# Down products of a macaron trunk as seven block products for eight

## The chip, the cores and the metric

The kernel runs on one core of a Trainium2 chip. The core has TensorE (PE) for matrix products, VectorE (DVE), ScalarE (ACT) and GpSimd (POOL) for element work, SyncE (SP) for issuing DMAs, an on-chip memory SBUF and an accumulator memory PSUM of eight banks. The metric is the device time of one launch in microseconds (us).

## The reference: what is computed

Two layers work on 528 tokens of width 1024 (512 frames behind 16 learned meta tokens). Each layer is

```
h = h + 1/2 * SwiGLU_1(RMSNorm(h))
h = h + mixer(RMSNorm(h))           # stick-breaking attention, a convolution branch, gates, output projection
h = h + 1/2 * SwiGLU_2(RMSNorm(h))
SwiGLU(x) = (silu(x @ w_gate) * (x @ w_up)) @ w_down     # inner width 2816
```

and after the layers a last RMSNorm, with the meta tokens dropped. All arrays are float32. The inner width 2816 is 22 row tiles of 128, the width 1024 is 8 tiles of 128. The change touches the four SwiGLU blocks (FFNs) alone, in them chiefly the product with `w_down`.

## The kernel before

Everything lies transposed: channels on the 128 partitions, tokens along the free dimension, so `h` is eight tiles of 128x528. In the last FFN only the 512 frame tokens are computed (mode `XO`), in the other three all 528 (`FULL`).

**Precision.** A float32 product is made of three products of a cheaper type: `split` (lines 77 to 80) gives a high part (a ScalarE copy) and the rest (a VectorE subtraction), for weights (`wh`, `wl`) and activations (`uh`, `ul` and so on), and every product is high x high, high x low, low x high. So each weight tile costs ScalarE and VectorE work before TensorE may use it.

**Weights.** The list `units` holds all weight pieces in the order of use. `unit` (line 243) hands the next one out and prepares ahead, `LOOK` = 3 units beyond it; raw tiles come by DMA on SP's queue into three buffers (`wr`), the two parts go into four buffers each (`wh`, `wl`). Mixer weights get their low part in another way: ScalarE writes the negated raw tile, and a DMA on Pool's queue adds the raw weights to it in memory (lines 224 to 226).

**Gate and up.** Row tiles of gate and up are computed in pairs by `quad` (line 566). Weights are cut into 2x2 blocks (two halves of the 1024 inputs by the two row tiles), activations into 2x2 blocks (input halves by token halves). Seven block products take the place of eight, and sums before and after make up for it: weight sums s1 and s3 are built by a DMA that loads one block and a DMA on Pool's queue that adds the other (`fetch_sums`, line 196), s2 and s4 by a VectorE addition (line 236). The results gather in PSUM: A (tag `ps`, two tiles), B (`pb`, one tile, begun as a ScalarE copy of A), G (copied to SBUF as q), E (`pe`, one tile, begun by VectorE as q - B), and c22 = q - B in SBUF. `out` (lines 592 to 594) makes u = up * silu(gate * rstd) of each quarter. The first tiles of an FFN (two, in the first FFN four) are made by plain products (line 502).

**Down.** The 22 row tiles lie in four groups of 4, 6, 6 and 6. After the quads of a group, `down` (line 622) multiplies its tiles by `w_down`, for all eight output tiles of the width (line 260). For this `parts` (line 484) has split each u into `ah` and `al`. In the first three groups VectorE takes an output from PSUM, times 1/2 and times the norm's factor rstd (line 638), and Pool adds it to `h` (line 640). In the last group Pool multiplies u by rstd beforehand (line 486), VectorE adds to `h` directly (line 633), and `after` prepares the next stage's input from each finished tile of `h`. The first two outputs of a group are interleaved so that the tiles that are ready latest are used last.

**Order.** TensorE takes products in the order written. The other engines' instructions are put in order by a planner from priorities (the order of writing, moved by `priority(offset)`), and each engine then runs its list in order and waits at its head. The mixer's TensorE order is written out by hand and isn't touched.

## Time and profile before

| quantity | value |
|---|---|
| time, median of 3 runs | 2152.11 us (2151.22 to 2152.19) |
| span of the profiled execution | 2150.5 us |
| the profiled execution's own time beside its span | not given apart from the span; the median of the runs is 1.6 us above it |
| busy: PE, DVE, ACT, POOL | 2135.9, 1521.5, 1137.9, 488.7 us |
| a quad of gate and up, FULL | 20.4 us |
| a down stage of six tiles, FULL | 35.1 us |
| moved by DMA | 324.90 MB |

In rows of the profile, `wl<-wr,wh 128x1024` means that a tile wl of 128 partitions by 1024 elements is written from wr and wh; `xN` is a count; "mean ns" is the duration of one; the text in square brackets of a time row is the engine's idle time before it and what ended it. A window's row gives the busy time of each engine in that stretch, then TensorE's granted clock, the DMA engines' busy share and GB/s.

### The profile page before, as it was taken

How to read it: one execution, taken by the hardware profiler on the slowest of the kernel's cores; microseconds unless marked ns; L12 is line 12 of the kernel's file. 1: busy time of each engine (PE TensorE's matmuls, PEld its weight loads, DVE VectorE, ACT ScalarE, POOL GpSimd, SP SyncE). 2: the span in 40 equal slices, each digit the busy share in tenths (PEclk: the TensorE clock that was granted, in tenths of full speed). 3: DMA queues.
4: the chain of work that ended last, by engine and by line, in shares of the span. 5: the costliest groups of instructions: out<-in, count | busy, mean ns of one | idle time of the engine just before them, and what ended most of it. 6: DMA issues, size and time to landing. Idle time of an engine off the chain costs nothing.

```text
span 2150.5 us, 39932 instructions
## 1 busy us (share of the span) xinstructions
PE 2135.9 (99%) x16226; PEld 2052.8 (95%) x16226; DVE 1521.5 (71%) x2091; ACT 1137.9 (53%) x1587; POOL 488.7 (23%) x449
## 2 busy tenths in 40 slices
PE   9999999999999999999999999999999999999998
PEld 9999999999999999999999999999888889999897
DVE  7867685677766777677877676856677767767685
ACT  6434355467776545343554443554778775444354
POOL 1322321211111131313113223212112111322320
PEclk9999999999999999999999999999999999999999
DMA  8465536865578747464365655368656886665542
GB/s 236 133 165 141 142 104 198 181 138 119 134 169 180 175 129 189 129 161 122 99 169 145 168 140 146 103 193 184 142 127 133 187 188 167 159 175 143 144 111 77
DMA packets 140168, 324.90 MB, mean 151 GB/s; under 512 B 15568, under 2 KB 19664, under 8 KB 139984
## 3 DMA queue, kind: packets, MB, share of 16 engines
q1 hardware_dynamic: 101856, 226.36, 33.3%
q0 software_dynamic: 37440, 95.44, 26.1%
q8 instruction: 127, 2.08, 0.4%
q10 hardware_dynamic: 688, 0.55, 0.1%
q14 instruction: 57, 0.47, 0.1%
HBM read 315.86 MB, written 6.42 MB: 150 GB/s over the span
## 4 chain that ended last, share of the span: by engine, by line
PE 99%; ACT 0%; DVE 0%; DMA 0%; issue 0%; DVEq 0%; ACTq 0%
PE pb L580 16%; PE ps L580 16%; PE ps L720 15%; PE ps L260 12%; PE ps L706 10%; PE pe L260 6%; PE pb L260 6%; PE pe L580 5%; PE z L706 2%; PE ps L502 2%; PE pe L502 1%; PE pb L502 1%; PE z L877 1%; PE po L921 1%; PE z L900 1%; PE ps L554 1%
## 5 line engine op out<-in xcount | busy, mean ns | idle before, releaser
L79 ACT CAST wh<-wr 128x1024 fp32r<-128x1024 f32 (+4 forms) x275 | 242.2, 887 | 372.4 <-PE ps L260 94.5
L80 DVE TENSOR_TENSOR wl<-wr,wh 128x1024 fp32r<-128x1024 f32 (+4 forms) x275 | 300.6, 1096 | 57.4 <-ACT wh L79 53.5
L79 ACT CAST wh<-s 128x1024 fp32r<-128x1024 f32 x158 | 165.8, 1049 | 274.9 <-DVE s L236 83.1
L80 DVE TENSOR_TENSOR wl<-s,wh 128x1024 fp32r<-128x1024 f32 x158 | 216.1, 1368 | 59.4 <-ACT wh L79 58.7
L720 PE MATMUL ps<-uh,wh 128*128 128x264 f32 (+1 forms) x792 | 243.8, 308 | 0.0
L720 PE MATMUL ps<-uh,wl 128*128 128x264 f32 (+1 forms) x792 | 240.0, 303 | 0.0
L720 PE MATMUL ps<-ul,wh 128*128 128x264 f32 (+1 forms) x792 | 239.9, 303 | 0.0
L640 POOL TENSOR_TENSOR h<-h,dt 128x528 f32<-128x528 f32 (+1 forms) x96 | 179.9, 1879 | 258.1 <-DVE dt L638 255.2
L210 POOL DMA_DIRECT2D s<-wg x78 | 72.8, 938 | 596.9 <-DMA s<-wg 337.9
L748 DVE SCALAR_TENSOR_TENSOR y<-uc,prm,y 128x528 f32<-128x528 f32 (+1 forms) x240 | 197.7, 824 | 4.1
L224 ACT CAST wh<-wr 128x1024 fp32r<-128x1024 f32 x104 | 109.1, 1049 | 141.2 <-issue 46.9
L580 PE MATMUL ps<-ul,wh 128*128 128x264 f32 (+1 forms) x624 | 177.4, 284 | 0.0
L580 PE MATMUL pb<-sl,wh 128*128 128x264 f32 (+1 forms) x624 | 176.9, 283 | 0.0
L580 PE MATMUL ps<-uh,wl 128*128 128x264 f32 (+1 forms) x624 | 176.9, 283 | 0.0
L580 PE MATMUL pb<-sh,wl 128*128 128x264 f32 (+1 forms) x624 | 176.8, 283 | 0.0
L580 PE MATMUL pb<-sh,wh 128*128 128x264 f32 (+1 forms) x624 | 176.5, 283 | 0.0
L580 PE MATMUL ps<-uh,wh 128*128 128x264 f32 (+1 forms) x624 | 176.2, 282 | 0.0
L720 PEld LDWEIGHTS ps<-uh,wl 128*128 128x128 f32 x792 | 149.1, 188 | 5.9
L720 PEld LDWEIGHTS ps<-uh,wh 128*128 128x128 f32 x792 | 148.9, 188 | 5.4
L720 PEld LDWEIGHTS ps<-ul,wh 128*128 128x128 f32 x792 | 149.0, 188 | 5.1
L260 PE MATMUL ps<-ah,wh 128*128 128x264 f32 (+1 forms) x616 | 142.0, 300 | 0.0
L260 PE MATMUL ps<-ah,wl 128*128 128x264 f32 (+1 forms) x616 | 141.8, 300 | 0.0
(319 smaller groups left out, 6460.8 us busy)
## 6 DMA issues: line engine op xcount, KB each, us to landing
wr<-wd SPq DMA_DIRECT2D x96, 384.0 KB, 3.6
wr<-win SPq DMA_DIRECT2D x72, 512.0 KB, 4.4
wl<-win POOLq DMA_DIRECT2D x72, 512.0 KB, 7.8
wr<-wg SPq DMA_DIRECT2D x117, 256.0 KB, 3.0
wr<-wu SPq DMA_DIRECT2D x117, 256.0 KB, 3.4
s<-wg SPq DMA_DIRECT2D x78, 256.0 KB, 5.2
s<-wu SPq DMA_DIRECT2D x78, 256.0 KB, 5.7
s<-wg POOLq DMA_DIRECT2D x78, 256.0 KB, 5.2
```

The source lines that it names most:

```text
L79: act.copy(hi, x)
L80: dve.tensor_tensor(out=lo, in0=x, in1=f(hi), op=ALU.subtract)
L210: pool.dma_start(t[:, a:b], src, accum_op=ALU.add)
L224: act.copy(hi[:, :nk], raw[:, :nk])
L260: pe.matmul(ps[:, c, :n], wt[:, k0 + k, :], xt[:, s:s + n], start=(k == 0 and pi == 0), stop=(k == end and pi == 2))
L502: pe.matmul(ps[:, e, :TH], wt[:, k, :], xt[:, s], start=(k == ORDER[0] and pi == 0), stop=(k == ORDER[-1] and pi == 2))
L554: pe.matmul(ps[:, e, :TH], wt[:, k, :], xt[:, s], start=(k == 0 and pi == 0), stop=(k == KD - 1 and pi == 2))
L580: pe.matmul(ps[:, e, :TH], wt[:, 4 * e + kk, :], xt, start=start and kk == 0 and pi == 0, stop=kk == 3 and pi == 2, skip_group_check=True)
L640: pool.tensor_tensor(out=tri(h[j], mode), in0=tri(h[j], mode), in1=tri(t, mode), op=ALU.add)
L706: pe.matmul(ps, wt[:, k0 + k, :], xt[:, s], start=(n == 0 and pi == 0), stop=(n == nk - 1 and pi == 2))
L720: pe.matmul(ps, wt[:, k, :], xt[:, s], start=(n == 0 and pi == 0), stop=(n == KD - 1 and pi == 2))
L748: t = dve.scalar_tensor_tensor(out=y, in0=uc[i][:, c0 + k:k + T], scalar=col(w0 + k), in1=y, op0=ALU.mult, op1=ALU.add)
```

## The change

- The groups become three of 6 tiles and one of 4. A pair of row tiles in `quad` is now tile i and tile i + 3 of a group (in the last group neighbours as before).
- In the first three groups `down_quads` takes the place of `down`: the six row tiles as two halves of three, the outputs as two halves of four, the tokens as two halves, seven products instead of eight, for two sets d of 2x2 output tiles. One product is 3 tiles x 3 parts x 2 output tiles = 18 matmuls of half the tokens. Weight sums are made as in `quad`, of 128x768, with loads of 1536 contiguous bytes per partition and output tile.
- The activations of a pair are split in seven halves: one half (`first_part`), one whole tile (`second_part`), and four half sums made by VectorE in place in the u tiles (`sum_ops`), split as two whole tiles (`sum_parts`) or, for the last pair of a group, one half at a time in the order of use (`sum_halves`). They stay in SBUF in 20 buffers (`ap`) and the `nsum` tile.
- u is multiplied by rstd beforehand in all groups, by Pool (`normed`), by VectorE for the last quarter of a group's last pair. `h` stays in SBUF throughout: an output leaves PSUM by ScalarE, times 1/2, and Pool adds its two half rows to `h` (`give`).
- Urgent operations get priority by `URGENT` = 200. The tags g, nt and dt share three buffers; s3, q and c22 have one buffer instead of two; the loads of s1 and s3 are issued apart from each other.
- The last group keeps `down`, with four tiles.

```diff
-GROUPS = ((0, 4), (4, 10), (10, 16), (16, 22))
-PLAIN, PLAIN_FIRST = 2, 4
+GROUPS = ((0, 6), (6, 12), (12, 18), (18, 22))
+NH = 3
+PAIRS = tuple(tuple((m0 + i, m0 + NH + i) for i in range(NH)) for m0, _ in GROUPS[:-1]) + (((18, 19), (20, 21)),)
+PLAIN, PLAIN_FIRST = 1, 2
...
+URGENT = 200
...
+    DOWN = ((0, "w11"), (1, "w11"), (0, "s1"), (0, "s2"), (0, "w21"), (0, "s3"), (0, "w22"), (0, "s4"),
+            (1, "s1"), (1, "s2"), (1, "w21"), (1, "s3"), (1, "w22"), (1, "s4"))
...
+                if gi < len(GROUPS) - 1:
+                    units += [((n, fi, l, ("d", gi, d)), (wd[l], m0, d), n) for d, n in DOWN]
+                else:
+                    units += [((f"d{fi}", l, gi, j), wd[l, j, :, m0:m1], m1 - m0) for j in ORDER]
...
+    SUM_BUFS = {"s1": 2, "s3": 1}
...
+            if is_down(n):
+                w, m0, d = src
+                j = 4 * c + 2 * d
+                return [(0, 2 * NH, w[j:j + 2, :, m0 + NH * k:m0 + NH * k + NH].rearrange("j p k c -> p j k c"))]
...
-            if nk == "w11":
-                fetch_sums()
+            size = 2 * NH if is_down(n) else 8
+            if nk in ("s1", "w22"):
+                fetch_sums("s1" if nk == "s1" else "s3")
             if nk in ("s2", "s4"):
-                x, y = raws[("s1", *at)], raws[("w22" if nk == "s2" else "w21", *at)]
+                x, y = (raws[(e, *at)][:, :size] for e in ("s1", "w22" if nk == "s2" else "w21"))
                 dve.tensor_tensor(out=x, in0=x, in1=y, op=ALU.add)
-            split(raws[("s1" if nk in ("s2", "s4") else nk, *at)], hi, lo)
+            raw = raws[("s1" if nk in ("s2", "s4") else nk, *at)][:, :size]
+            split(raw, hi[:, :size], lo[:, :size])
...
+                return fp.tile([P, T], F32, tag="nt", bufs=3, name="g")
...
+            def normed(eng, u, s):
+
+                eng.tensor_tensor(out=u[:, s], in0=u[:, s], in1=norm["r"][:, s], op=ALU.mult)
...
             def parts(u, m):
-                if m >= GROUPS[-1][0]:
-                    pool.tensor_tensor(out=tri(u, mode), in0=tri(u, mode), in1=tri(norm["r"], mode), op=ALU.mult)
-                ah = fp.tile([P, T], F32R, tag="ah", bufs=6, name="ah")
-                al = fp.tile([P, T], F32R, tag="al", bufs=6, name="al")
+                normed(pool, u, both)
+                ah, al = (fp.tile([P, T], F32R, tag="ap", bufs=20, name=n) for n in ("ah", "al"))
...
+            def first_part(p, ua):
+                t = two(slot(p, 0), mode)
+                split(ua[:, toks[0]], t[:, 0], t[:, 1])
+                a_parts["w11", p] = (t[:, 0], t[:, 1])
+
+            def whole_part(p, n, u, names):
+                hi, lo = slot(p, n), slot(p, n + 1)
+                split(tri(u, mode), tri(hi, mode), tri(lo, mode))
+                for name, s in zip(names, toks):
+                    a_parts[name, p] = (hi[:, s], lo[:, s])
+
+            def second_part(p, ub):
+                whole_part(p, 1, ub, ("w21", "s4"))
+
+            def sum_ops(ua, ub):
+
+                t1, t2 = toks
+                return ((ub[:, t2], ua[:, t2], ub[:, t2], ALU.subtract), (ua[:, t2], ua[:, t1], ua[:, t2], ALU.subtract),
+                        (ua[:, t1], ub[:, t2], ua[:, t1], ALU.subtract), (ub[:, t1], ub[:, t1], ua[:, t1], ALU.add))
+
+            def sum_halves(p, ua, ub):
+
+                places = (("s1", 3, 1), ("s3", 5, 1), ("s2", 5, 0), ("w22", 3, 0))
+                tiles = {n: slot(p, n) for n in range(3, 7)}
+                ops = sum_ops(ua, ub)
+                for n in (0, 1, 2, 3):
+                    o, x, y, op = ops[n]
+                    name, at, t = places[n]
+                    dve.tensor_tensor(out=o, in0=x, in1=y, op=op)
+                    a_parts[name, p] = tuple(tiles[at + e][:, toks[t]] for e in range(2))
+                    split(o, *a_parts[name, p])
+
+            def sum_parts(p, ua, ub):
+                for o, x, y, op in sum_ops(ua, ub):
+                    dve.tensor_tensor(out=o, in0=x, in1=y, op=op)
+                whole_part(p, 3, ub, ("w22", "s1"))
+                whole_part(p, 5, ua, ("s2", "s3"))
...
                 B = ptile("pb")
-                act.copy(v(B), v(A))
+                with priority(-URGENT):
+                    act.copy(v(B), v(A))
                 G = ptile()
                 products(G, "s1", sx(0), True)
-                q = sp.tile([P, 2, TH], F32, tag="q", bufs=2, name="q")
-                act.copy(q, v(G))
-                while late:
-                    parts(*late.pop())
+                q = sp.tile([P, 2, TH], F32, tag="q", bufs=1, name="q")
+                with priority(-URGENT):
+                    act.copy(q, v(G))
                 products(B, "s2", sx(1))
                 E = ptile("pe")
-                dve.scalar_tensor_tensor(out=v(E), in0=v(B), scalar=-1.0, in1=q, op0=ALU.mult, op1=ALU.add)
+                with priority(-URGENT):
+                    dve.scalar_tensor_tensor(out=v(E), in0=v(B), scalar=-1.0, in1=q, op0=ALU.mult, op1=ALU.add)
+                while late:
+                    late.pop()()
                 products(A, "w21", x(0, 1))
                 out(A, 0, 0)
+                if not last:
+                    normed(pool, u[0], toks[0])
                 products(B, "s3", sx(2))
-                c22 = sp.tile([P, 2, TH], F32, tag="c22", bufs=2, name="c22")
-                dve.scalar_tensor_tensor(out=c22, in0=v(B), scalar=-1.0, in1=q, op0=ALU.mult, op1=ALU.add)
+                c22 = sp.tile([P, 2, TH], F32, tag="c22", bufs=1, name="c22")
+                with priority(-URGENT):
+                    dve.scalar_tensor_tensor(out=c22, in0=v(B), scalar=-1.0, in1=q, op0=ALU.mult, op1=ALU.add)
                 products(E, "w22", sx(3))
+                if not last:
+                    first_part(p, u[0])
                 out(c22, 1, 1)
                 out(E, 1, 0)
-                parts(u[1], m + 1)
+                if last:
+                    parts(u[1], m + 1)
+                else:
+                    normed(pool, u[1], both)
                 products(B, "s4", x(1, 1))
-                out(B, 0, 1)
-                late.append((u[0], m))
-
-            def down(gi, tp=None):
+                with priority(-URGENT):
+                    out(B, 0, 1)
+                if last:
+                    late.append(lambda: parts(u[0], m))
+                elif p < NH - 1:
+                    normed(pool, u[0], toks[1])
+                    late.append(lambda: (second_part(p, u[1]), sum_parts(p, *u)))
+                else:
+                    late.append(lambda: (second_part(p, u[1]), normed(dve, u[0], toks[1]), sum_halves(p, *u)))
+
+            def down_quads(sp, gi):
+                with priority(-URGENT):
+                    late.pop()()
+
+                def products(ps, name, d, start=False):
+                    hi, lo = unit(name, fi, l, ("d", gi, d))
+                    for k in range(NH):
+                        xh, xl = a_parts[name, k]
+                        for pi, (wt, xt) in enumerate(((hi, xh), (hi, xl), (lo, xh))):
+                            for e in range(2):
+                                pe.matmul(ps[:, e, :TH], wt[:, NH * e + k, :], xt, start=start and k == 0 and pi == 0,
+                                          stop=k == NH - 1 and pi == 2, skip_group_check=True)
+
+                def v(t):
+                    return t[:, :, :TH]
+
+                def give(src, c, t, d):
+
+                    dt = two(fp.tile([P, T], F32, tag="nt", bufs=3, name="dt"), mode)
+                    with priority(-URGENT):
+                        act.activation(dt, src, AF.Copy, scale=0.5)
+                    for e in range(2):
+                        hj = h[4 * c + 2 * d + e][:, toks[t]]
+                        pool.tensor_tensor(out=hj, in0=hj, in1=dt[:, e], op=ALU.add)
+
+                def opposite(out, B, q):
+                    with priority(-URGENT):
+                        dve.scalar_tensor_tensor(out=out, in0=v(B), scalar=-1.0, in1=q, op0=ALU.mult, op1=ALU.add)
+
+                As = []
+                for d in range(2):
+                    As.append(ptile())
+                    products(As[d], "w11", d, True)
+                for d, A in enumerate(As):
+                    B = ptile("pb")
+                    with priority(-URGENT):
+                        act.copy(v(B), v(A))
+                    G = ptile("pe")
+                    products(G, "s1", d, True)
+                    q = sp.tile([P, 2, TH], F32, tag="q", bufs=1, name="q")
+                    with priority(-URGENT):
+                        act.copy(q, v(G))
+                    products(B, "s2", d)
+                    E = ptile("pe")
+                    opposite(v(E), B, q)
+                    products(A, "w21", d)
+                    give(v(A), 0, 0, d)
+                    products(B, "s3", d)
+                    c22 = sp.tile([P, 2, TH], F32, tag="c22", bufs=1, name="c22")
+                    opposite(c22, B, q)
+                    products(E, "w22", d)
+                    give(c22, 1, 1, d)
+                    give(v(E), 1, 0, d)
+                    products(B, "s4", d)
+                    give(v(B), 0, 1, d)
+
...
-                    t = fp.tile([P, T], F32, tag="nt", bufs=3, name="dt")
-                    dve.scalar_tensor_tensor(out=sv(t, mode), in0=pv(pd, mode), scalar=0.5, in1=sv(norm["r"], mode),
-                                             op0=ALU.mult, op1=ALU.mult)
-                    pool.tensor_tensor(out=tri(h[j], mode), in0=tri(h[j], mode), in1=tri(t, mode), op=ALU.add)
+                    dve.scalar_tensor_tensor(out=sv(h[j], mode), in0=pv(pd, mode), scalar=0.5, in1=sv(h[j], mode),
+                                             op0=ALU.mult, op1=ALU.add)
...
+                for gi, group in enumerate(PAIRS):
+                    for p in range((PLAIN_FIRST if first else PLAIN) if gi == 0 else 0, len(group)):
+                        quad(sp, gi, p)
                     if gi < len(GROUPS) - 1:
-                        down(gi)
+                        down_quads(sp, gi)
```

The start of the first FFN and the plain start of the others hand their tiles to the same functions; the last FFN's squares use a shared buffer.

131 lines of the change are left out of this document (76 added, 55 removed).

## The prediction

> **What bounds the kernel now.** I read the page's head first, then whom TensorE waits for, then the chain of waits, then the stages by windows.
>
> ```profile
> span 2150.5 us, 39932 instructions
> ...
> PE 2135.9 (99%) x16226; PEld 2052.8 (95%) x16226; DVE 1521.5 (71%) x2091; ACT 1137.9 (53%) x1587; POOL 488.7 (23%) x449
> ...
> PE 99%; ACT 0%; DVE 0%; DMA 0%; issue 0%; DVEq 0%; ACTq 0%
> ```
> ```profile
> PE ps L554 <- ACT wh L79: 4.8, 1, 4.8
> ```
> The end is set by TensorE alone: the chain stays on it, and its only wait of note is the 4.8 us before the first product. So a change is worth the matmul time it takes out, less the new holes it makes. The chain in order of time gives the price of a matmul:
>
> ```profile
> 368.33 5.83 PE z L706 x48
> ...
> 839.09 5.82 PE ps L580 x48
> ...
> 1052.41 8.78 PE ps L260 x72
> ...
> 1087.56 5.83 PE pb L502 x48
> ...
> 1898.72 5.69 PE ps L580 x48
> ...
> 1918.62 8.34 PE ps L260 x36
> ```
> A 264-column matmul costs 0.121 us (5.82/48) in block products (line 580) and 0.122 in down products (line 260). In the last FFN, where the meta tokens are dropped, a 256-column one costs 0.1185 and a 512-column one 0.2317. The windows show what else is loaded while TensorE runs full at clock 1.00: a quad of a middle group, a quad of the last group, a down stage, the start of the next FFN.
>
> ```profile
> 915.10:935.50 20.40, 20.40 (x171) 20.40 (x170) 16.13 (x22) 10.81 (x16) 3.24 (x4) 1.00 0.62 160
> 1011.50:1032.00 20.50, 20.50 (x171) 20.50 (x170) 18.22 (x22) 11.15 (x16) 3.51 (x2) 1.00 0.32 86
> 955.96:991.10 35.14, 35.14 (x290) 35.14 (x290) 19.58 (x21) 8.41 (x11) 13.99 (x7) 1.00 0.36 104
> 1060.50:1091.50 31.00, 31.00 (x256) 31.00 (x255) 30.96 (x49) 22.54 (x36) 0.00 (x0) 1.00 0.37 116
> ```
> After span, columns are PE, PEld, DVE, ACT, POOL. VectorE is second: 16 to 18 of 20.4 us in a quad, and wholly busy for 31 us between two FFNs without one hole in TensorE.
>
> **The change, part by part. TensorE.** Per FFN the down products of 18 tiles in a full FFN were 8x18x6 = 864 matmuls; they become 3 groups of 14 products of 18, 756. 108 fewer at 0.1213 are 13.1 us, three times: 39.3. In the last FFN 8x22x3 = 528 of 512 columns (122.3 us) become 756 of 256 (89.6) and 96 of 512 (22.2): 10.5. Together 49.8 us. Gate and up keep their 39 quads. The matmul count doesn't move: 3x108 fewer, 324 more.
>
> **VectorE in a quad.** Its prices are the spacing of starts where it doesn't wait:
>
> ```profile
> 916.06 1.22 DVE L236 TENSOR_TENSOR s<-s,wr 128x1024 f32<-128x1024 f32 x1
> 917.20 0.70 DVE L80 TENSOR_TENSOR al<-up,ah 128x528 fp32r<-128x528 f32 x1
> 917.81 0.43 DVE L594 TENSOR_TENSOR up<-pb,g 128x264 f32<-128x264 f32 x1
> 918.16 1.22 DVE L80 TENSOR_TENSOR wl<-wr,wh 128x1024 fp32r<-128x1024 f32 x1
> 919.29 1.22 DVE L80 TENSOR_TENSOR wl<-s,wh 128x1024 fp32r<-128x1024 f32 x1
> ```
> ```profile
> 854.46 0.96 DVE L80 TENSOR_TENSOR wl<-wr,wh 128x768 fp32r<-128x768 f32 x1
> 855.34 0.43 DVE L592 TENSOR_TENSOR g<-c,rstd 128x264 f32<-128x264 f32 x1
> ```
> So 1.14 for 1024 columns, 0.88 for 768, 0.62 for 528, 0.35 for 264. A quad now takes nine of 1.14, four of 0.62 and eight of 0.35: 15.5. The change replaces two residual splits (1.24) by one half split, three whole ones and four half sums (0.35 + 1.86 + 1.40 = 3.6): 17.9. To this comes Pool, which now multiplies both row tiles by the norm (2x264 and 528 columns). What that does, the last group shows already:
>
> ```profile
> 1012.41 1.33 POOL L486 TENSOR_TENSOR up<-up,rstd 128x528 f32<-128x528 f32 x1 [2.46 <-DVE up L594]
> 1015.93 2.18 POOL L486 TENSOR_TENSOR up<-up,rstd 128x528 f32<-128x528 f32 x1 [2.19 <-DVE up L594]
> ```
> ```profile
> 1012.52 2.31 DVE L236 TENSOR_TENSOR s<-s,wr 128x1024 f32<-128x1024 f32 x1
> ...
> 1016.84 2.35 DVE L80 TENSOR_TENSOR wl<-s,wh 128x1024 fp32r<-128x1024 f32 x1
> ```
> Beside a Pool operation of 1.33 a VectorE one of 1.22 takes 2.31 to 2.35: they go one after the other. Two of them made the quad's VectorE time 18.22 instead of 16.13, 2.1 more. So the second and third quad of a group need 17.9 + 2.1 = 20.0 of TensorE's 20.4. The first of a group needs 3.3 less, 16.7: what is left of a pair (second split, sums) is issued inside the next quad, and the third pair's goes to the down stage.
>
> **VectorE in a down stage**, which lasts 252x0.1213 = 30.6 us. 14 weight splits and 4 weight sums at 0.88, 4 opposites at 0.62: 18.3; the last pair's rest, with its own norm, 3.9. The outputs cost it nothing more: they go by ScalarE (14 weight casts, 4 copies and 8 outputs by the rows below: 14x0.84 + 12x0.59 = 18.8 of 30.6 us).
>
> ```profile
> L79 ACT CAST wh<-wr 128x768 fp32r<-128x768 f32 x96 | 79.1, 836 | 162.1 <-PE ps L260 48.9 <-issue 38.8 <-PE pe L260 27.9
> ...
> L603 ACT COPY q<-ps 128x528 f32<-128x528 f32 x29 | 17.2, 592 | 0.0
> ```
> But Pool adds 16 halves of 264 columns. Such an operation isn't in the trace: between half of 1.33 and all of it; I take 0.7, nearest in work to the half. That is 11.2 us, of which between none and all delays VectorE; I take 7, since some two thirds of its stage is on operations of two SBUF inputs. Then 29.2 of 30.6. A group of three quads and a down stage: 16.7 + 2x20.0 + 29.2 = 85.9 of TensorE's 91.8 us. It fits, at 94%, with little room in three of four stages. I charge holes between 0 and 6.6 us a group (the upper end is the slow rival's, below) and take 0.9, nearer the bottom because the 31 us of full VectorE above made no hole: 12 groups, 10.8.
>
> **Shared pair.** The Trainium skill, "SBUF — State Buffer", section "SBUF: two separate sides", has this pair of ports as an exclusive lock held for a whole instruction, the later one blocked fully. The 2.31 and 2.35 agree. By it all of Pool's time would fall on VectorE whenever that is never idle, which is the slow rival.
>
> **Last group, four tiles instead of six.** The first two outputs start with the tiles that are ready, which covers the last quad's late rest. Cover falls from 60 matmuls (7.3 us) to 36 (4.4).
>
> ```profile
> 1052.45 0.43 DVE L592 TENSOR_TENSOR g<-pb,rstd 128x264 f32<-128x264 f32 x1 [0.86 <-PE pb L580]
> ...
> 1057.85 0.71 DVE L80 TENSOR_TENSOR al<-up,ah 128x528 fp32r<-128x528 f32 x1 [2.10 <-ACT ah L79]
> ...
> 1060.49 0.71 DVE L633 SCALAR_TENSOR_TENSOR h<-ps,h 128x528 f32<-128x528 f32 x1 [1.93 <-PE ps L260]
> ...
> 1090.13 0.76 DVE L319 SCALAR_TENSOR_TENSOR ul<-h,prm,uh 128x528 fp32r<-128x528 f32 x1
> ```
> The rest was ready at 1058.6, 6.2 after the stage began at 1052.4: 1.8 late, unless the new priority of that output hastens it. 0 to 1.8, take 0.9, four times: 3.6.
>
> **Into the mixer (twice).** The stage's outputs now take 24 matmuls (2.9 us) each instead of 36 (4.4), and weights are prepared three units ahead.
>
> ```profile
> 355.05 1.06 ACT L224 CAST wh<-wr 128x1024 fp32r<-128x1024 f32 x1 [2.13 <-PE ps L260]
> ```
> ```profile
> 357.36 0.88 POOL L226 DMA_DIRECT2D wl<-win  x1 [19.30 <-ACT wl L225]
> ```
> ```profile
> DMA to landing us min/median/max: 8.0/8.2/8.9
> ```
> The first mixer weight began at 355.05, 13.3 before its use at 368.33; its low part was issued at 357.36 and landed 8.2 to 8.9 later, near 366. Three units are now 8.8 us, 4.5 less, so it lands about 2.2 late, with 0.5 covered by the high products: 0 to 2.2, take 1.7, twice: 3.4.
>
> **Between the FFNs (once).** VectorE had 31 us of work from 1060.5; the last input half (1090.13) was done at 1090.9 and needed at 1087.56 + 7/8x5.83 = 1092.7. TensorE now comes 11.7 earlier; VectorE starts 2.9 earlier and saves about 2.3 (eight weight splits a third shorter than 0.88): late by 5 at most, 0 if the deferred sums give way; take 2.6.
>
> **Loads and queues.** A down stage issues 14 transfers of 384 KB for 8, four of them accumulations on Pool's queue. Each accumulation waits there until its plain load has landed; behind it stand the output adds, which hold the three tiles of the tag that outputs, g tiles and sums now share, and for these ScalarE's outputs wait. Four outputs come in 15 us and the adds of one last 1.4, so a block of 4 us on Pool is covered; the cost if not is in the handover rival. The single q and c22 cost nothing: their last readers are done a product or more before the next write, behind w11 and s1. The single s3 buffer leaves six products, 13.1 us, between the two output pairs of a down stage, for a 384 KB load and its accumulation; the 512 KB accumulation above takes 8.2 and
>
> ```profile
> wr<-wd SPq DMA_DIRECT2D x96, 384.0 KB, 3.6
> ```
> makes 11.8; issue adds some 1 to 2. A delay of 1 us is hidden by the three products of preparation; uncovered it is 12 us in all, one per group. I take nothing.
>
> **Sum**: 2150.5 - 49.8 + 10.8 + 3.6 + 3.4 + 2.6 = 2121.1. The page gives this execution only its span; the median of the runs, 2152.11, lies 1.6 above, and I add that: 2122.7.
>
> **The rivals.** *Nearly all hidden* (0.18): only the mixer's entry costs: 2152.1 - 49.8 + 3.4 = 2105.7. For it: the full 31 us without a hole. Against: Pool's blocking was not there.
>
> *Handovers in the down stage* (0.13): a product now covers 18 matmuls, 2.2 us, where a quad's had 2.9. In that time the opposite must read the one pb tile: an operation under way (0.9, or up to 2.3 when blocked) and its own 0.7. Three such places in each of 24 output pairs, 0.5 us each, are 36 instead of 10.8: 2147.9. For it: one pb and one pe tile. Against: the new priorities put these operations first.
>
> *VectorE becomes the bound* (0.16): the slower side. If every Pool operation blocks it (2.8 in a quad, 11.2 in a down stage) and a quarter of the 4.3 us it idles in the 915.1 quad can't be filled, the second and third quads take 21.8 instead of 20.4 and the down stage 34.4 instead of 30.6: 2.8 + 3.8 = 6.6 a group, 79 in all: 2150.5 - 49.8 + 9.6 + 79 + 1.6 = 2190.9. It decides from a need above 20.4 a quad; I put it at 20.0. The lock rule above makes this time if it is read strictly.
>
> *The matmuls saved aren't time saved* (0.03): the 3024 new block matmuls would have to cost 0.0165 more each, 0.138, to eat the 49.8; at half of that the time is 2147.6. Against: lines 260 and 580, one with banks in alternation as here, cost 0.122 and 0.121.
>
> **How the numbers follow.** The forecast has 0.50: 2122.7, its own range 2108 to 2142. Some 0.2% (4 us) is about what the measurement tells from none. Faster takes the forecast, the hidden case and half of the handovers and of the last rival: 0.76; within 0.2%: 0.07, from their other halves; slower: 0.17. For 8 in 10 the range reaches from 2104 to 2158, leaving out the bottom of the hidden case and most of the VectorE-bound one.
>
> **What would show it.** PE still x16226 with some 2086 us of work; DVE about 2415 instructions; down stages of 30.6 to 33 us; waits of TensorE on VectorE of 1 us and less, most in the second and third quads and at the opposites. Wrong: quads above 21 us (VectorE bound), down stages above 34, or a mixer entry without a hole.

## The result, and the profile after

The changed kernel takes 2311.47 us (2302.48 to 2318.72, four runs) against 2151.66 for the kernel before beside it: ratio 1.074, 95% interval 1.0712 to 1.0767. The prediction said 2122.7, 2104 to 2158. The sign is wrong and the time is far outside the range.

The head of the page of the changed kernel, and the first line of its chain of work:

```profile
span 2316.9 us, 41061 instructions
...
PE 2164.1 (93%) x16214; PEld 2077.1 (90%) x16214; DVE 1739.5 (75%) x2415; ACT 1299.4 (56%) x1899; POOL 648.0 (28%) x676
...
PE 21%; DVE 4%; DMA 3%; issue 2%; ACT 1%; POOL 1%; POOLq 0%; SPq 0%; DVEq 0%; ACTq 0%
```
VectorE has exactly the 2415 instructions of the forecast. But TensorE is idle for 2316.9 - 2164.1 = 152.8 us, where the forecast's sum leaves 2121.1 - 2086.1 = 35.0, and busy for 2164.1 instead of some 2086. The two differences, 117.8 and 78.0, make up all of 2316.9 - 2121.1 = 195.8.

Next, busy times by stage for one group of the second FFN: its three quads, then its down stage. Kernel before:

```profile
798.10:859.40 61.30, 61.30 (x507) 61.30 (x506) 48.33 (x61) 31.06 (x43) 13.40 (x14) 1.00 0.68 171
859.40:894.50 35.10, 35.10 (x289) 35.10 (x289) 19.54 (x21) 8.29 (x11) 14.01 (x7) 1.00 0.35 109
```
The changed kernel (the columns are the stretch, its length, busy time and instructions of TensorE, its weight loads, VectorE, ScalarE and Pool, the granted clock, the DMA share, GB/s):

```profile
885.70:960.40 74.70, 66.50 (x506) 66.08 (x505) 53.88 (x73) 33.83 (x49) 27.54 (x26) 0.91 0.62 143
960.40:994.90 34.50, 32.89 (x255) 32.48 (x254) 26.08 (x34) 19.38 (x30) 19.29 (x19) 0.95 0.67 175
```
In this group the time is lost in the gate and up quads, whose products the change leaves as they were: 74.7 us for 61.3. The down stage, which it rewrites, takes 34.5 for 35.1. VectorE is busy for 53.88 of the 74.7, so it isn't full. The clock is 0.91 in the quads.

The waits of TensorE in the changed kernel (us in total, times, longest):

```profile
PE pb L672 <- ACT pb L692: 76.5, 27, 5.6
PE pe L742 <- ACT ap L82: 20.2, 12, 2.4
PE pb L742 <- DVE pe L759: 9.4, 9, 1.5
PE pb L742 <- ACT pb L768: 5.4, 4, 2.4
```
Half of the idle time is one wait: a quad's s2 product waits for ScalarE's copy of the tile A into the tile B. Two large waits of other engines lead there:

```profile
POOL s L235 <- DMA s<-wg: 217.2, 34, 28.2
ACT ap L82 <- POOL up L513: 198.3, 68, 6.4
```
Pool stands before an accumulation until its plain load has landed, and ScalarE stops for Pool's multiplication of u by rstd. One such place in the changed kernel, by its timeline, in order of time (the bracket is the idle time just before, and what ended it):

```profile
170.82 1.20 POOL L235 DMA_DIRECT2D s<-wd  x1 [6.91 <-DMA s<-wd]
171.56 1.25 POOL L513 TENSOR_TENSOR up<-up,rstd 128x264 f32<-128x264 f32 x1
172.84 0.41 ACT L82 CAST ap<-up 128x264 fp32r<-128x264 f32 x1 [5.02 <-POOL up L513]
173.16 0.42 ACT L106 ACTIVATE g<-g 128x264 f32<-128x264 f32 x1
173.29 0.43 DVE L83 TENSOR_TENSOR ap<-up,ap 128x264 fp32r<-128x264 f32 x1 [4.13 <-ACT ap L82]
178.44 2.85 POOL L513 TENSOR_TENSOR up<-up,rstd 128x528 f32<-128x528 f32 x2 [5.64 <-DVE up L686]
180.62 0.63 ACT L82 CAST ap<-up 128x528 fp32r<-128x528 f32 x1 [2.20 <-POOL up L513]
182.11 0.59 ACT L692 COPY pb<-ps 128x528 f32<-128x528 f32 x1
182.75 0.59 PE L672 MATMUL pb<-sh,wh 128*128 128x264 f32 x1 [4.23 <-ACT pb L692]
```
Pool waits 6.91 us for a plain load, because the next thing in its queue is the accumulation onto it. The multiplication behind it starts at 171.56, and ScalarE has stood 5.02 us at the split that reads the product. Behind that split stand the silu at 173.16 and, in the end, the copy. Later in the quad the second tile takes the way VectorE, Pool, ScalarE with a Pool that had nothing to do: 2.20 us more at ScalarE's head. Of these 7.2 us some 3.0 are absorbed, and 4.23 become a hole in TensorE.

This place is not a single case. In the first three FFNs the timeline has 14 quads in which a wait behind an accumulation (4.0 to 6.4 us) and a second one of 2.2 us come before the same copy. In each of them TensorE's hole is the sum of the two less 2.9 to 3.0 us; together these holes are 61.2 of the 76.5 us. In the last group of each FFN a wait of 2.1 to 2.2 us comes alone before a copy, and no hole follows.

After the hole TensorE's matmuls are slow. The same place in stretches of 3 us:

```profile
179.00:182.00 3.00, 0.00 (x0) 0.00 (x0) 1.49 (x4) 1.38 (x2) 2.29 (x2) 0.79 0.00 0
182.00:185.00 3.00, 2.25 (x10) 2.25 (x11) 2.97 (x4) 2.17 (x4) 0.00 (x0) 0.50 0.21 26
185.00:188.00 3.00, 3.00 (x17) 3.00 (x17) 1.99 (x4) 0.63 (x1) 0.00 (x0) 0.57 0.77 243
188.00:191.00 3.00, 3.00 (x27) 3.00 (x26) 2.80 (x4) 1.62 (x3) 1.19 (x1) 1.00 0.45 134
```
In 185 to 188 it is busy throughout and does 17 matmuls; in 188 to 191 it does 27. The mean clock of the run is 0.970, against 0.999 before. Over the span that is (0.999 - 0.970) x 2316.9 = 67 us, but part of it falls on time in which TensorE did nothing, as from 179 to 182. The trace has 28 stretches of half clock, 141 us together, and TensorE is busy in 116 us of them. So the lower clock costs some 58 of the 78 us of longer matmuls. The Trainium skill, "TensorE: Matmul & The Clock Gate", section "Part 1: The HAM clock gate (the "warmup" mystery)", has the clock go to half after at least one idle window of some 3.4 us, and run what is issued in about the first 3.4 us after it at that half. The rows agree on the half, 0.50 and later 1.00, but not on the times. From 179 to 182 a mean of 0.79 means half clock from about 180.7, only 2.2 us after TensorE's last matmul (182.75 - 4.23 = 178.52); and the half lasts until about 187.6, 4.8 us after work resumed. In this run all 14 holes of 3.8 us and more were followed by a stretch of half clock, and about half of the 14 holes between 1.6 and 3.2 us were too.

### The profile page after: what moved, and what is told of

It reads as the page before. It is cut to its first block, busy times and chain, and to the rows that moved or that the text cites. A ratio compares the mean times of both kernels' runs of the same rounds, so it can differ in the third digit from the quotient of the medians.

```text
span 2316.9 us, 41061 instructions
## 1 busy us (share of the span) xinstructions
PE 2164.1 (93%) x16214; PEld 2077.1 (90%) x16214; DVE 1739.5 (75%) x2415; ACT 1299.4 (56%) x1899; POOL 648.0 (28%) x676
## 2 busy tenths in 40 slices
DMA packets 172048, 353.28 MB, mean 152 GB/s; under 512 B 16720, under 2 KB 63824, under 8 KB 171856
## 5 line engine op out<-in xcount | busy, mean ns | idle before, releaser
L83 DVE TENSOR_TENSOR wl<-s,wh 128x1024 fp32r<-128x1024 f32 (+1 forms) x254 | 345.5, 1360 | 69.6 <-ACT wh L82 68.0
L82 ACT CAST wh<-s 128x1024 fp32r<-128x1024 f32 (+1 forms) x254 | 245.8, 968 | 240.1 <-DVE s L262 82.9
L82 ACT CAST wh<-wr 128x1024 fp32r<-128x1024 f32 (+4 forms) x251 | 222.2, 888 | 115.0 <-PE ps L672 36.2
L672 PE MATMUL pb<-sh,wh 128*128 128x264 f32 (+1 forms) x624 | 196.0, 314 | 78.9 <-ACT pb L692 76.5
L82 ACT CAST ap<-up 128x264 fp32r<-128x264 f32 (+3 forms) x168 | 87.0, 520 | 292.0 <-POOL up L513 198.3
L513 POOL TENSOR_TENSOR up<-up,rstd 128x528 f32<-128x528 f32 (+3 forms) x107 | 150.0, 1413 | 310.2 <-DVE up L686 256.9
L672 PEld LDWEIGHTS pb<-sh,wh 128*128 128x128 f32 x624 | 131.9, 211 | 86.6 <-ACT pb L692 82.7
L755 POOL TENSOR_TENSOR h<-h,dt 128x264 f32<-128x264 f32 (+1 forms) x192 | 201.3, 1385 | 19.8 <-ACT dt L752 19.8
L83 DVE TENSOR_TENSOR ap<-up,ap 128x264 fp32r<-128x264 f32 (+3 forms) x168 | 94.6, 564 | 142.9 <-ACT ap L82 142.5
L262 DVE TENSOR_TENSOR s<-s,wr 128x1024 f32<-128x1024 f32 (+1 forms) x126 | 163.1, 1294 | 1.4
```

Source lines behind the costliest of these rows:

```text
L82: act.copy(hi, x)
L83: dve.tensor_tensor(out=lo, in0=x, in1=f(hi), op=ALU.subtract)
L262: dve.tensor_tensor(out=x, in0=x, in1=y, op=ALU.add)
L513: eng.tensor_tensor(out=u[:, s], in0=u[:, s], in1=norm["r"][:, s], op=ALU.mult)
L672: pe.matmul(ps[:, e, :TH], wt[:, 4 * e + kk, :], xt, start=start and kk == 0 and pi == 0, stop=kk == 3 and pi == 2, skip_group_check=True)
L755: pool.tensor_tensor(out=hj, in0=hj, in1=dt[:, e], op=ALU.add)
```

## The experiments

Four theories. *Queue*: Pool's products stand in its queue behind accumulations that wait for their plain loads, and all that is behind ScalarE's split waits with it. *Hop*: the way VectorE, Pool, ScalarE costs at ScalarE's head even when Pool is free. *Capacity*: Pool's operations hold VectorE until VectorE is the bound. *Handover*: the shorter down products wait for the copies and opposites between them. The kernel before took 2151.3 to 2152.1 us beside each of them. Where no interval is given, the time is that of a single run.

**The norm taken off Pool**, at this place and in the seven other calls like it outside the last group.

```diff
-                normed(pool, ua, both)
+                normed(dve, ua, both)
```


> The changed kernel, with u multiplied by rstd on VectorE instead of Pool in the first three groups; everything else as it is. Queue theory (Pool's norm stands behind accumulations that wait for their plain loads, ScalarE waits at its head for the split of that u, and the copy into pb, which TensorE needs, stands behind that): the 76.5 us of TensorE waiting for the pb copy go below 15, the half-clock stretches after holes mostly go with them, time 2130 to 2190. Theory that VectorE's capacity with Pool's blocking is the bound: VectorE now does 1.3 us more a quad instead of being blocked for 2.1, need about 19.2 of 20.4, so the time falls by less than 40 us, 2270 or more. Handover theory: the down stages keep their holes and the time stays above 2250.

Measured: 2155.86 us, 156 us less than the changed kernel, though VectorE has more to do. TensorE's wait for the copy is almost gone:

```profile
PE pb L672 <- ACT pb L692: 8.1, 10, 2.5
```
Capacity and handover fall as main causes: VectorE does more, the down stages still have their products, and Pool still has its 192 additions. Queue and hop are both left, since this edit takes both away.

**No norm at all** (the multiplication by rstd is left out in the first three groups).

> The changed kernel without the multiplication of u by rstd in the first three groups (that part of the computation is left out). Queue theory: as with the norm on VectorE or a little better, 2120 to 2180. Capacity theory: VectorE's need falls from 20.0 to 17.9 a quad, down stages keep Pool's adds: 2150 to 2230, with the holes left in the down stages. Handover theory: above 2250.

Measured: 2165.16 us, in the range of the queue theory and in that of the capacity theory too. With VectorE relieved of the operation as well, it is no faster than the run before, so VectorE's added work is not what is left there. Why it is some 9 us slower isn't settled; it is one run of each.

**The kernel before, with Pool's multiplication.** All tiles of u are multiplied on Pool, and the down output goes without the factor.

```diff
-                if m >= GROUPS[-1][0]:
-                    pool.tensor_tensor(out=tri(u, mode), in0=tri(u, mode), in1=tri(norm["r"], mode), op=ALU.mult)
+                pool.tensor_tensor(out=tri(u, mode), in0=tri(u, mode), in1=tri(norm["r"], mode), op=ALU.mult)
```


> The kernel before, with one part of the change alone: Pool multiplies u by rstd in all groups (and the output of a group leaves out that factor in return). Queue theory: the norm stands behind Pool's accumulations here too, ScalarE waits at its head for the split, the pb copy is late: TensorE waits for it 30 to 100 us, time 2180 to 2260. Capacity theory: VectorE's need is 16.1 + 2.1 = 18.2 of 20.4 a quad, as the last group's quads already show without a hole: 2150 to 2160.

Measured: 2167.21 us. The same ScalarE wait is there:

```profile
ACT ah L79 <- POOL up L485: 151.7, 86, 3.7
```
Yet it costs only 16 us: between the expectations of the theories. Of these 86 waits only 7 (18.7 us) stand behind an accumulation; the others are the hop alone. So the hop needs company to hurt.

**Accumulations issued later**: for s1 three unit preparations behind its plain load, for s3 two.

```diff
-                fetch_sums("s1" if nk == "s1" else "s3")
+                fetch_sums("s1" if nk == "s1" else "s3", LATER[nk])
```


> The changed kernel, with the accumulating DMA of s1 issued three units of weight preparation after its plain load and that of s3 two units after, so that Pool meets it when the plain load has landed; same work on every engine. Queue theory: Pool's waits for plain loads (217 + 162 us) fall by more than half, the pb-copy waits fall below 40 us, time 2150 to 2250; what is lost again would show as ScalarE waiting for DMA on the sums. Capacity theory: no engine's work changes, so 2300 to 2320. Handover theory: 2290 to 2320.

Measured: 2306.93 us, no change. Pool's waits for the loads hardly fell and ScalarE's not at all:

```profile
ACT ap L82 <- POOL up L526: 196.9, 68, 6.4
```
So this edit did not take the cause away; it says nothing against the queue theory.

To weigh the two, ScalarE's waits for Pool's product in the changed kernel were counted one by one in the timeline, and sorted by what Pool did before that product. Over all groups there are 80, 217.9 us together: 61 with a Pool that had itself waited for VectorE's u (127.7 us, 2.1 each), 19 behind an accumulation (90.2 us, 4.7 each). (The expectation of the run with ScalarE's order fixed, below, mixes this count with the total of 198.3.) Three runs against each other:

**The first split emitted later**, for the first two quads of a group.

```diff
-                if not last:
+                if p == NH - 1 and not last:
                     first_part(p, u[0])
...
-                    late.append(lambda: (second_part(p, u[1]), sum_parts(p, *u)))
+                    late.append(lambda: (first_part(p, u[0]), second_part(p, u[1]), sum_parts(p, *u)))
```


> Everything of the changed kernel stays: Pool multiplies u by rstd, adds the outputs and issues the accumulations. Only the split of the first quarter of u is emitted later: for the first two quads of a group it comes in the next quad, together with the splits that are late already, so no ScalarE split stands ahead of the silus and copies of the same quad. Hop theory (ScalarE stops at the head of its queue because a split waits for Pool's product, and the silu and the copy behind it keep TensorE waiting): ScalarE's wait for Pool's products falls from 198.3 us to under 100 and the time to 2170 to 2230. Queue theory (Pool is held by its accumulations for longer than a quad): the late splits wait as well, 2260 to 2320. Capacity theory (Pool and VectorE slow each other): no change, 2290 to 2330.

Measured: 2313.7 us, ScalarE's wait 210.9 us. By the numbers expected this is the queue theory, or capacity. But ScalarE's order in the run shows that the planner put the late splits ahead of the next quad's copy all the same: a later place in the program didn't make them later on the engine. The run can't judge the hop.

**ScalarE's order fixed**, by a dependency without a wait: `hold` puts every split of a part behind instruction i on ScalarE.

```diff
+            def hold(i, part, *a):
+                behind.append(i)
+                part(*a)
+                behind.clear()
...
-                    first_part(p, u[0])
                 out(c22, 1, 1)
-                out(E, 1, 0)
+                silu = out(E, 1, 0)
+                    hold(silu, first_part, p, u[0])
...
-                    late.append(lambda: (second_part(p, u[1]), sum_parts(p, *u)))
+                    late.append(lambda i: (hold(i, second_part, p, u[1]), sum_parts(p, *u)))
```


> All operations of the changed kernel stay, Pool's norm too; ScalarE's order alone is fixed: the split of a quad's first quarter of u comes behind the silu of the same quad's third output, and the split of u's second tile behind the copy into q of the next quad (but for the last quad of a group, whose second tile is needed at once). In the changed kernel 61 of ScalarE's 74 waits for Pool's product end at a Pool that itself had nothing to do until VectorE gave u, 128 of 198 us; 19 stand behind an accumulation, 70 us. Hop theory (a ScalarE that stops for two engines in a row, with silus and copies behind it, is the cause): ScalarE's wait falls below 110 us, the time to 2170 to 2240. Queue theory (the waits behind accumulations, up to 6 us each, are the cause): 2270 to 2315.

**No accumulations.**

```diff
-        for a, b, src in pieces(n, "w12"):
-            pool.dma_start(into(t, n, a, b), src, accum_op=ALU.add)
```


> The accumulating transfers of the sums s1 and s3 are left out (s1 and s3 are then plain blocks, so this part of the computation is missing, and 28 MB and more of traffic with it); Pool multiplies and adds as in the changed kernel, but waits for no transfer. Queue theory: 2150 to 2220, and ScalarE's wait for Pool's products well below 100 us. Hop theory: the waits with an idle Pool stay, 2240 to 2300.

Measured: 2199.42 with the order fixed, 2192.82 without accumulations. Waits with the order fixed:

```profile
PE pe L753 <- ACT ap L84: 26.8, 11, 2.8
...
PE pb L682 <- ACT pb L703: 6.2, 8, 1.8
...
ACT ap L84 <- POOL up L518: 39.4, 21, 3.3
```
Waits without accumulations:

```profile
PE pb L670 <- ACT pb L690: 8.0, 9, 4.1
...
ACT ap L82 <- POOL up L511: 119.0, 60, 4.5
```
Each edit alone takes TensorE's 76.5 us of waits for the copy down to 6 to 8, and 112 to 119 us off the time. Each time lies in the range of the theory whose part was taken away, so both theories are right and neither is enough. The queue theory missed in the second kernel in that ScalarE's wait is 119.0, not well below 100. That kernel keeps 60 such waits, all with a Pool that no accumulation held, and TensorE hardly sees them: by themselves 2 us fit into its slack, as they nearly do in the kernel before (above). In the one with the order fixed Pool still waits for its loads (147.3 us for s blocks of the gate weights alone), but ScalarE stops for only 39.4 us of it, and the copies behind are in time. What costs is their sum in one quad, 7.2 us in the place shown, against a slack of some 3. And the holes that the sum makes bring the lower clock with them. (The second kernel also moves less, 293.46 MB in place of 353.28; how much of its gain is that was not tried.)

**Outputs taken out by VectorE**, the norm left on Pool.

```diff
-                    with priority(-URGENT):
-                        act.activation(dt, src, AF.Copy, scale=0.5)
-                        pool.tensor_tensor(out=hj, in0=hj, in1=dt[:, e], op=ALU.add)
+                        with priority(-URGENT):
+                            dve.scalar_tensor_tensor(out=hj, in0=src[:, e], scalar=0.5, in1=hj, op0=ALU.mult, op1=ALU.add)
```


> The output of a down quad is taken out by VectorE in one operation (h = 0.5 x psum + h) instead of ScalarE's copy and two additions on Pool; the norm stays on Pool. Hop theory: the wait of ScalarE for Pool's products stays near 200 us, and with it the time, 2270 to 2320. Theory that Pool's runs of additions are what harms (they hold VectorE for 4 us, and stand ahead of the next group's accumulations): 2150 to 2220, and the wait of TensorE for the copy into pb falls below 30 us.

Measured: 2262.91 us. ScalarE's wait stays (186.3 us) as the hop theory said, but the time is lower than it allowed: the outputs' way through ScalarE and Pool has a price of its own, 49 us here. The edit takes 192 additions off Pool and 96 copies off ScalarE, and no run tells the two apart.

**Both moves**, the norm and the outputs on VectorE.

> Both moves together: VectorE multiplies u by rstd and takes the outputs out, Pool has only its accumulations and the norm of the last group. By the rows VectorE then has 19.2 us of a quad's 20.4 and 27.2 of a down stage's 29.2, with nothing on Pool to stand beside it. Hop theory: like the run with the norm alone on VectorE, 2156, less what its additions still cost: 2120 to 2156. Theory that a full VectorE becomes the bound: 2160 to 2220.

> The kernel with both moves, in more rounds: 2133 to 2139 us, that is 0.6 to 0.9% below the kernel before. Were the one look luck, it would be within 0.2% of it.

Measured: 2135.79 us in the first run, and 2139.06 in five more (2137.81 to 2144.22), ratio to the kernel before 0.9944, interval 0.993 to 0.9958. That is 0.4 to 0.7% faster than the kernel before, just above the range of the second expectation. The page's line of busy times, and two stretches of the second FFN, the first from its first quad to the end of its down products, the second the quads of one group:

```profile
PE 2102.1 (98%) x16214; PEld 2025.8 (95%) x16214; DVE 1728.6 (81%) x2698; ACT 1255.2 (59%) x1803; POOL 350.6 (16%) x393
```
```profile
750.00:1074.00 324.00, 321.96 (x2625) 319.95 (x2624) 285.48 (x438) 175.46 (x255) 50.23 (x50) 1.00 0.65 162
...
822.30:883.60 61.30, 61.30 (x506) 61.30 (x505) 55.16 (x84) 33.94 (x48) 10.54 (x11) 1.00 0.76 183
```
VectorE is busy 55.16 of 61.3 us, with no hole. "VectorE becomes the bound" falls once more: TensorE's 61.30 us are those of the kernel before. The same FFN before:

```profile
754.20:1087.40 333.20, 333.20 (x2739) 333.20 (x2738) 241.50 (x303) 149.85 (x209) 83.61 (x62) 1.00 0.51 137
```
**What Pool's work costs besides.** With ScalarE's order fixed the time is still 44 us above that of the kernel with the norm on VectorE. Two kernels with the second tile of a group's last quad multiplied by VectorE, one of them with the outputs on VectorE too:

```diff
-                    normed(pool, u[1], both)
+                    normed(pool if p < NH - 1 else dve, u[1], both)
```


> The kernel with ScalarE's order fixed, and beside that the second tile of u of the last quad of a group is multiplied by VectorE, since there its split is wanted at once and can't be put behind anything; Pool still multiplies the other tiles and adds the outputs. Theory that what is left of the loss is that same hop at the end of a group (TensorE's 26.8 us of waits for the split, 11 times, and the lower clock behind them): 2150 to 2170. Theory that it is Pool's operations as such: 2185 to 2200.

> The last kernel, and the outputs taken out by VectorE in one operation; Pool keeps the multiplications of all quads but the last of a group. VectorE then needs some 17.9 us of the 20.4 of a first or second quad and 19.2 of a last one. If Pool's multiplications are harmless once nothing waits for them at ScalarE's head: 2125 to 2140, as good as the kernel with all of them on VectorE (2139) or better. If they slow VectorE by the share in which both run: 2140 to 2160.

Measured: 2192.15, and 2172.45 us (ratio 1.01, interval 1.0083 to 1.0117). The first is where it was expected from Pool's operations as such, in part by luck, as the next runs show; the second is above both expectations. TensorE still waited 15.9 and 15.5 us for the split in the last quad. That could be the fix itself, which holds the first split of that quad back. So in two more kernels that quad has its early split again, and all of its norm on VectorE:

```diff
-                    normed(pool, u[0], toks[0])
+                    normed(pool if p < NH - 1 else dve, u[0], toks[0])
...
+                if not last and p == NH - 1:
+                    first_part(p, u[0])
                 out(c22, 1, 1)
                 silu = out(E, 1, 0)
-                if not last:
+                if p < NH - 1 and not last:
```


> As the kernel with the second tile of the last quad multiplied by VectorE, but in the last quad of a group the first quarter too, and its split back at its early place; Pool still multiplies in the first two quads and adds the outputs. If the order fixed in the last quad is what makes TensorE wait for the split there (15.9 us, 11 times): that wait goes below 4 us and the time falls to 2165 to 2180. If what is left is VectorE held by Pool's operations: the time stays at 2185 to 2195.

> The last kernel, and the outputs taken out by VectorE. If Pool's multiplications in the first two quads cost nothing but what they make ScalarE wait: 2135 to 2148, like the kernel with all of it on VectorE (2139). If they hold VectorE, and that reaches TensorE: 2155 to 2172, little below the 2172 of the kernel with the last quad's early split still late.

Measured: 2174.56, and 2151.34 us (ratio 1.0006, interval 0.9996 to 1.0016). The wait for the split fell in both, in the first to

```profile
PE pe L755 <- ACT ap L84: 3.9, 7, 0.9
```
and the time by 18 and 21 us, as the first kernel's expectation had it: that part was the fix's own. The rest goes with Pool's operations. With the last quad's norm on VectorE, the way of the outputs over ScalarE's copy and Pool's additions costs 2174.6 - 2151.3 = 23 us; in the kernels with all of the norm on VectorE, 2155.9 - 2139.1 = 17. The kernel with Pool's multiplications in the other two quads is 2151.3 - 2139.1 = 12 us slower than the one without them; it also has ScalarE's order fixed, which the other has not, so the 12 are not Pool's for certain. The second kernel missed both of its expectations: it lies between "nothing" and "little below 2172".

What Pool's operations do to VectorE shows in its subtractions. The one for s blocks in the changed kernel, in the one with the norm moved, and in the one with both moved:

```profile
L83 DVE TENSOR_TENSOR wl<-s,wh 128x1024 fp32r<-128x1024 f32 x158 | 231.1, 1463 | 48.3 <-ACT wh L82 47.2
```
```profile
L83 DVE TENSOR_TENSOR wl<-s,wh 128x1024 fp32r<-128x1024 f32 x158 | 226.1, 1431 | 38.1 <-ACT wh L82 35.3
```
```profile
L83 DVE TENSOR_TENSOR wl<-s,wh 128x1024 fp32r<-128x1024 f32 x158 | 193.2, 1223 | 33.1 <-ACT wh L82 25.4 <-PE ps L577 4.0 <-PE ps L672 2.0
```
1223 ns where Pool has only transfers and the last group's norm, 1431 with the additions beside them, 1463 with the rest of the norm too.

## Why the prediction was wrong, step by step

*TensorE, -49.8: held in the main.* In the kernel with both moves the FFN above is 108 matmuls shorter by count of the program and 324.0 us long for 333.2. The saving worked out was 13.1; 3.9 go to holes and slower matmuls, 1.3 a group. Over the whole kernel less of it is seen: TensorE's busy time falls by 2135.9 - 2102.1 = 33.8 us.

*VectorE in a quad and in a down stage: held.* The charge for Pool's blocking was 3 x 2.1 + 7 = 13.3 us a group. Measured: VectorE's splits and sums of weights, 1024 and 768 long, are together 115 us longer in the changed kernel than in the one with both moves, over 12 groups 9.6. In the group shown VectorE is busy 53.88 us in the three quads and 26.08 in the down stage, where the prediction had 56.7 and 29.2.

*Holes of 0.9 a group, from 0 to 6.6: wrong, and the bound too.* What the changed kernel loses beyond the sum is 117.8 + 78.0 us, or 16 a group if all of it is put down to the 12 groups. The upper bound was taken from one mechanism, a full VectorE, and so could not contain this one. With both moves TensorE is idle for 2136.9 - 2102.1 = 34.8 us in all, against the forecast's 35.0. That agreement is partly luck: the waits in its groups are less than was charged and those between the FFNs more (below). Its matmuls are 16 us longer than forecast; half clock explains some 3 of them, the rest is open.

*Loads and queues: this is the step that failed.* It said of an accumulation in Pool's queue: "behind it stand the output adds", "a block of 4 us on Pool is covered", and "I take nothing". The output adds were one thing behind it. The multiplications by rstd were the other, and they were costed only as time that Pool takes from VectorE. The blocks are 4.7 us on the mean where they reach ScalarE, near the 4 that was assumed, so the size was about right. What was left out is who waits: ScalarE's split stops for the product, and a silu, a copy and TensorE's next product stand behind the split. "Covered" was judged for this block alone; in the quads above it came to 4.0 to 6.4 us and met 2.2 us of hop, against a slack of 3. The profile of before showed this hop already, in the last group, where Pool multiplied u even then:

```profile
ACT ah L79 <- POOL up L486: 33.0, 24, 2.5
```
The prediction quoted two neighbours of it for other ends: Pool's multiplication with its own 2.19 us of idle time, and VectorE at 1057.85 waiting 2.10 us for ScalarE's split.

*The clock: not in the sum.* Every hole was charged at its length. In this run 152.8 us of idle TensorE brought some 58 us of slower matmuls with them.

*The single s3 buffer, "a delay of 1 us is hidden": roughly right.* There is a late load now and then, such as the one that ScalarE meets here in the last FFN; TensorE then waits 2.45 us for the copy behind it, and all its waits for that copy are 5.4 us in the whole run. Two buffers for s3 were not tried. The late load:

```profile
2124.97 0.83 ACT L82 CAST wh<-s 128x768 fp32r<-128x768 f32 x1 [3.24 <-DMA s<-wd]
```
*Last group, 3.6: held.* TensorE's waits for the splits there are 2.3 + 0.9 = 3.2 us, in both the changed kernel and the one with both moves.

*Into the mixer, 3.4: the size about right, the cause not.* In the kernel with both moves TensorE waits 2.5 us at the two entries, for parts of the mixer's input and of its norm. None of its listed waits is for a mixer weight.

*Between the FFNs, 2.6: too small.* TensorE has one wait of 5.1 us there, in both the changed kernel and the one with both moves. In the latter the lower clock behind it costs some 3 us more:

```profile
1074.00:1105.30 31.30, 25.80 (x187) 25.32 (x186) 27.28 (x45) 17.84 (x29) 5.29 (x6) 0.89 0.69 169
```
*The rivals.* The only one on the slower side, VectorE as the bound, had its sign right and its mechanism wrong, at 2190.9. "Quads above 21 us" was named as a sign of it; the quads came to 24.9, from another cause. "Down stages above 34" came true as well, at 34.5. Handovers in the down stage: small, 9.4 + 5.4 us of waits. (In the chances the other halves come to 0.08, not 0.07, which leaves 0.16 for slower; nothing hangs on it.)

## What to carry to other kernels

When an operation is moved to another engine, follow its result as well as its cost: who reads it, at which place in an in-order queue, and what stands behind that reader. Count, too, everything that the new engine already waits for ahead of it in its queue. Delays that are each covered add up within one period against one slack, so bound the sum. Charge a long TensorE hole (here 3.8 us and more) with the slow matmuls behind it as well. To take such a chain away, put its middle on the engine that makes its input (here the norm on VectorE, 156 us), or fix the order of the engine that waits (112 us), before shortening any operation.

## What the runs showed of the hardware

A VectorE operation can be held longer than one Pool operation. In the changed kernel six additions of Pool ran back to back, and one VectorE subtraction of 1.22 us lasted through all that was left of them:

```profile
2140.70 4.50 POOL L755 TENSOR_TENSOR h<-h,dt 128x256 f32<-128x256 f32 x6
2141.49 4.80 DVE L83 TENSOR_TENSOR wl<-s,wh 128x1024 fp32r<-128x1024 f32 x1 [1.17 <-ACT wh L82]
```
It ended at 2146.29, 1.09 us after the last addition (2145.20). The Trainium skill, "SBUF — State Buffer", section "SBUF: two separate sides", has the pair of ports held for the whole of an instruction by whichever starts first. Read for one instruction at a time, that would end the wait with the addition under way, 4.50 / 6 = 0.75 us here; the rows show a run of Pool's operations keeping the ports. It is no single case: in the changed kernel 18 of VectorE's splits and sums of weights took 4.2 to 6.2 us, each beside five to seven of Pool's operations, and in the kernel with both moves none took more than 1.23.
